# Scoring both maps of a query tile together, with their low-part products on two halves of the matrix array

## The chip, the cores and the metric

The kernel runs on one core of one Trainium2 chip. The metric is the device time of one launch in microseconds (us). TensorE (PE in the rows) does the matmuls and loads their weights (PEld); VectorE (DVE), ScalarE (ACT) and GpSimd (POOL) do the rest; SyncE (SP) starts transfers.

## The reference, cut to what matters

One inference step of two layers over 1,024 latent tokens and 128 context tokens. Each layer projects, mixes (four heads of differential attention, a Fourier branch, a gated branch) and projects back. The change sits in the attention of the latent tokens:

```python
def _diff_attention(q, k, v, lam, subln_w, lam_init):
    s = jnp.einsum('bhqmd,bhkmd->bhmqk', q, k,
                   preferred_element_type=jnp.float32) * (HEAD_DIM ** -0.5)
    p = jax.nn.softmax(s, axis=-1)
    a = p[:, :, 0] - lam * p[:, :, 1]
    o = jnp.einsum('bhqk,bhke->bhqe', a, v.astype(jnp.float32))
    ...
```

A head has two maps `m`, each with queries and keys of 64 dimensions. 1,024 queries see 1,152 keys (128 cached ones and the 1,024 latent tokens).

## The kernel before, in words

**Two-part numbers.** Matmuls run on `float32r` operands, and each operand is split into a high part (its rounding to `float32r`) and a low part (the rest). A product is then high by high, high by low and low by high.

**Scores.** For a head and a map, `K[:, m]` holds the high parts of the 64 key dimensions in one half of the 128 rows and the low parts in the other half (`split_k`, L435 to L440). `Q[:, m]` holds the high part of the query twice, in both halves (`pack`, L615 to L622). One matmul of `Q` by `K` over 128 rows thus gives two of the three products. The third, low query by high key, uses `qlo`, which holds the low part in the half where the keys' high parts stand and zeros in the other half (`low`, L625 to L630), so it too runs over 128 rows. `score` (L632) makes one map of one tile of 128 queries: three matmuls of 384 keys with `Q`, three with `qlo`, all added up in a PSUM tile `S` of three banks (L638). Then VectorE takes the negated maximum (`nm`, L640), and ScalarE the exponential and its sum (`P`, L642).

**From scores to values.** `softmax_diff` (L583 to L585): a reciprocal on VectorE, one scaling of the second map on GpSimd (`P`, L584), one multiply-and-add on VectorE (`P`, L585). `transpose` (L652): nine transposes into a PSUM tile `T`, read by ScalarE (high part, L655) and VectorE (low part `a`, L656). `values` (L662), once for two tiles: 27 matmuls into a PSUM tile `pv`, finished by `finish_o` (L594 to L604).

**PSUM.** `S`, `T` and `pv` take turns in a ring of two buffers of three banks each (`psS`), so each waits until the one before the last has been read. The other two banks (`psM`) are a ring of two for the projections' `z` and for small tiles.

**The order on TensorE** is written out by hand (`manual_schedule`). `attention` is a generator which goes over 32 tiles of a layer (eight for each of four heads). In step n it scores tile n, takes the values of a finished pair if there is one (odd n), and transposes tile n-1. At each `yield` the loop around it puts in "fill": groups of three matmuls (486 in its own units) of the projections `z` of the next heads, later of the other branches (`zt`). `FILL` is the amount for each head, `SHARE` the factor for each kind of place. `fill.until` puts in all that is missing of a projection that a head needs. At the same places one step of a head's small context attention (`prompt`, tiles `sp`, `atp`, `pvp`) is put in from the list `side`, and from the third head on `MFILL` units of modulation work on VectorE. The other engines' orders come from a scheduler, which puts what is marked `high_priority` first.

Of the kernel before, what the change touches and what calls it, by code (L numbers as in the profile page):

```python
# [10 lines left out]
F32 = mybir.dt.float32  # L11
# [12 lines left out]
CH = 384  # L24
# [5 lines left out]
SWAP = [k ^ 16 for k in range(32)]  # L30

PACE = 2
SHARE = [0.75, 1.25, 1, 1]
EARLY, LATE = 200, 0
MODS_POOL = (1, 4, 7)
MHEAD = 2
MFILL = 450
TAIL = 4
START_X = (1, 2, 0, 0, 0, 0, 0, 6)
START_W = (0, 0, 1, 2, 0, 0, 0, 0)  # L40
# [8 lines left out]

X_TAGS = {"wr": ("wraw", "woraw", "wada", "tabr", "mr", "ba"), "z": ("zz", "sh", "gt", "vT", "gmt", "gmg", "fot", "vs", "bd", "pqp", "ws", "kc", "vc", "Pp", "modacc"), "Q": ("Q", "bdr", "wsr", "h32"),
          "sq": ("sq", "wft", "dftp", "msq", "bds", "cb")}
X_BUFS = {"wr": 2, "z": 3, "Q": 2, "sq": 3, "X": 2}
X_TAGS = {n: t for t, names in X_TAGS.items() for n in names}

# [1 line left out]
def f(ap):  # L58
    return ap.bitcast(F32)
# [3 lines left out]
def backbone_step(ctx, tc, xs, xp, cT, w_ada, b_ada, w_in, w_out, ckT, cv, lamv, wf, wsT, bsT,  # L63
# [61 lines left out]
    neglam = cp.tile([128, L], F32, name="neglam")  # L125
    subs = cp.tile([128, L], F32, name="subs")

    qlo = [cp.tile([128, 2, 128], F32R, name=f"qlo{i}") for i in range(2)]
    qps = [cp.tile([128, 2, 128], F32, name=f"qp{i}") for i in range(2)]
    for t in qlo + qps:  # L130
        pool.memset(t if t.dtype == F32 else f(t), 0.0)

    def silu_c():
        sp.dma_start(cb, cT)
# [245 lines left out]
    def mm_dims(w, c, late=None):  # L380

        z = psM((128, CH), "z")
        n = 0
        for kt in range(KT):
            for a, b in ((0, 0), (0, 1), (1, 0)):
                pe.matmul(z, lhsT=w[:, a, kt, :], rhs=Hc[c][:, b, kt, :], start=n == 0, stop=n == 23)  # L386
                n += 1
            if kt == 3 and late:
                late()
            yield 486  # L390
        return z

    def mm_tok(w, ts):
# [122 lines left out]
        def chunk(self, c, z):  # L516
            silu_to(self.gs[:, c * CH:(c + 1) * CH], z, tX([128, CH], "gt"))

    finished = set()

    class Units:

# [84 lines left out]
    class Head:  # L607
# [7 lines left out]
        def pack(self, p):  # L615

            qr, qs = self.qr, slice(p * 256, p * 256 + 256)
            Q = self.Q = tX([128, 2, 256], "Q", F32R)
            act.activation(Q[0:64, 0], qr[0:64, qs], AF.Copy)
            act.activation(Q[64:128, 0], qr[0:64, qs], AF.Copy)  # L620
            act.activation(Q[64:128, 1], qr[64:128, qs], AF.Copy)
            act.activation(Q[0:64, 1], qr[64:128, qs], AF.Copy)  # L622
            return Q

        def low(self, i, Q):  # L625

            ql = slice((i % 2) * 128, (i % 2) * 128 + 128)
            for m in range(2):
                r = slice(64 * m, 64 * m + 64)
                pool.tensor_tensor(qlo[i % 2][r, m], self.qr[r, i * 128:(i + 1) * 128], f(Q[r, m, ql]), op=ALU.subtract)  # L630

        def score(self, Q, i, m, zz):  # L632
            S, K = psS(), self.K
            ql = slice((i % 2) * 128, (i % 2) * 128 + 128)

            for e, q in enumerate((Q[:, m, ql], qlo[i % 2][:, m])):
                for n in range(3):
                    pe.matmul(S[:, n, :CH], lhsT=q, rhs=K[:, m, n * CH:(n + 1) * CH], start=e == 0, stop=e == 1)  # L638
            nm = small([128, 1], "nm", 4)
            dve.tensor_reduce(nm, S[:, :, :CH], axis=AX.XY, op=ALU.max, negate=True)  # L640
            P = tP(name="P")
            act.activation(P.rearrange("p (c k) -> p c k", c=3), S[:, :, :CH], AF.Exp, bias=nm,  # L642
                           accum_out=zz[:, m:m + 1])
            return P

        def transpose(self, i, a):
            if i % 2 == 0:
# [22 lines left out]
        def prompt(self):  # L670

            l = self.l
            nm = small([128, 2], "nmp", 2)
            zz = small([128, 2], "zzp", 2)
            P = tX([128, 2, 128], "Pp")
            for m in range(2):
                S = psM((128, 128), "sp")
                pe.matmul(S, lhsT=self.qp[:, m], rhs=self.kp, start=True, stop=True)
                dve.tensor_reduce(nm[:, m:m + 1], S, axis=AX.X, op=ALU.max, negate=True)
                act.activation(P[:, m], S, AF.Exp, bias=nm[:, m:m + 1], accum_out=zz[:, m:m + 1])  # L680
                yield 0.5 * PACE
# [7 lines left out]
            pv = psM((128, 2, 128), "pvp")  # L689
            pe.matmul(pv[:, 0], lhsT=self.vp, rhs=aT, start=True, stop=True)  # L690
            sq = square_o(pv[:, 0], 128)
            yield 0.5 * PACE
            finish_o(l, pv[:, 0], pv[:, 1], sq, 128, self.gs, slice(SEQ_S, TOK))

    def attention(l, fill):

# [4 lines left out]
        for n in range(8 * H + 2):  # L701
            h, i = min(n // 8, H - 1), n % 8
            if n < 8 * H:
                if i == 0:
                    fill.until((l, U_K + h), (l, U_Q + h), (l, U_V + h))
                    hd = Head(l, h)
                    Qn = hd.pack(0)
                    hd.low(0, Qn)
                if i % 2 == 0:
                    Q = Qn  # L710
                zz = small([128, 2], "zz2", 4)
                with tc.high_priority(offset=EARLY):
                    p1 = hd.score(Q, i, 0, zz)
                if i < 7:
                    hd.low(i + 1, Qn)
                with tc.high_priority(offset=EARLY):
                    side.fill(1)
                yield h, 0
                with tc.high_priority(offset=EARLY):
                    p2 = hd.score(Q, i, 1, zz)  # L720
                if i % 2 == 0 and i < 6:
                    Qn = hd.pack(i // 2 + 1)
                with tc.high_priority(offset=EARLY):
                    side.fill(1)
                yield h, 1
            if done:
                if done[1] == 0:
                    fill.until((l, U_G + done[0].h))
                    done[0].begin_values()
                with tc.high_priority(offset=EARLY):  # L730
                    finish = done[0].values(done[1])
                with tc.high_priority(offset=EARLY):
# [421 lines left out]
```

## Time and profile before

| | |
|---|---|
| median of 3 runs | 1440.45 us (1434.82 to 1440.82) |
| the profiled execution | 1439.59 us, of which the span from first to last instruction is 1437.7 us |
| TensorE busy in the span | 93% |
| VectorE, ScalarE, GpSimd busy | 63%, 52%, 55% |
| mean granted TensorE clock | 0.979 |

The span leaves out 1.9 us of the execution. A busy TensorE counts pipelined matmuls from their start to a modelled end, so its spacing from start to start says more than its busy time.

### The profile page before, as it was taken

The numbers are of one execution on the slowest core, as the hardware profiler recorded it, in microseconds if no ns is written. First come the engines' busy times: TensorE is split into PE (matmuls) and PEld (weight loads), VectorE is DVE, ScalarE is ACT, GpSimd is POOL, SyncE is SP. The second block draws the span as 40 slices with busy tenths as digits, with TensorE's granted clock in tenths as the row PEclk, the third lists the DMA queues.
The fourth block names the chain that finished last, engine by engine and source line by source line (L and its number), as shares of the span: only waits on it lengthen the run. The fifth ranks groups of instructions, "written<-read, shape, count | busy, mean of one in ns | idle before, by whom it ended". The sixth has DMA issues, their size and how long they took to land. (4 is left out here: it accounts for less than half of the span.)

```text
span 1437.7 us, 21298 instructions
## 1 busy us (share of the span) xinstructions
PE 1330.9 (93%) x8264; PEld 1236.6 (86%) x8264; DVE 907.6 (63%) x1354; ACT 746.6 (52%) x1380; POOL 793.4 (55%) x723
## 2 busy tenths in 40 slices
PE   6899998889899999999997989989799999999997
PEld 4689998879788998987887989988789999998786
DVE  3646667787877865355785565668775684435576
ACT  3576666557454444353656565755565544435320
POOL 2455657567563446336687676575575343533752
PEclk9999999999999999999999999999999999999999
DMA  9310102211220221363341100112020010126432
GB/s 337 147 49 17 35 18 65 75 46 36 88 76 22 98 74 42 108 211 114 124 161 45 50 19 32 49 44 80 32 65 3 30 47 30 47 78 221 154 133 80
DMA packets 56158, 114.43 MB, mean 80 GB/s; under 512 B 4973, under 2 KB 32493, under 8 KB 55929
## 3 DMA queue, kind: packets, MB, share of 16 engines
q1 hardware_dynamic: 56056, 113.07, 23.7%
q8 instruction: 65, 1.06, 0.3%
q14 instruction: 37, 0.30, 0.1%
HBM read 95.47 MB, written 17.58 MB: 79 GB/s over the span
## 5 line engine op out<-in xcount | busy, mean ns | idle before, releaser
L386 PE MATMUL z<-H,w 128*128 128x384 f32 x2520 | 499.8, 345 | 22.4 <-DVE V L506 5.0
L386 PEld LDWEIGHTS z<-H,w 128*128 128x128 f32 x2520 | 444.9, 193 | 29.0 <-ACT vT L492 4.9
L642 ACT ACTIVATE P<-S,nm 128x1152 f32<-128x1152 f32 x128 | 156.4, 1222 | 118.6 <-DVE nm L640 112.1
L640 DVE TENSOR_REDUCE nm<-S 128x1 f32<-128x1152 f32 x128 | 172.3, 1349 | 40.4 <-PE S L638 39.9
L401 PE MATMUL zt<-whi,H 128*128 128x256 f32 x1152 | 158.7, 285 | 4.8 <-ACT ug L767 3.4
L401 PEld LDWEIGHTS zt<-whi,H 128*128 128x128 f32 x1152 | 147.0, 192 | 7.5 <-ACT ug L767 4.0
L584 POOL TENSOR_SCALAR P<-P,rz,neglam 128x1152 f32<-128x1152 f32 x64 | 86.8, 1356 | 98.3 <-DVE rz L583 87.2
L585 DVE SCALAR_TENSOR_TENSOR P<-P,rz 128x1152 f32<-128x1152 f32 x64 | 105.2, 1643 | 42.3 <-POOL P L584 42.3
L630 POOL TENSOR_TENSOR qlo<-qr,Q 64x128 fp32r<-64x128 f32 x128 | 81.4, 641 | 86.8 <-PE S L638 80.2
L367 POOL TENSOR_TENSOR w<-wraw,w 128x1024 fp32r<-128x1024 f32 x36 | 89.6, 2489 | 65.4 <-ACT w L366 64.9
L638 PE MATMUL S<-K,Q 128*128 128x384 f32 x384 | 93.2, 351 | 21.4 <-DVE a L656 11.0
L662 PE MATMUL pv<-a,V 128*128 128x256 f32 x864 | 109.2, 283 | 3.1 <-ACT P L642 3.1
L662 PEld LDWEIGHTS pv<-a,V 128*128 128x128 f32 x864 | 106.6, 191 | 5.1 <-ACT P L642 5.1
L656 DVE TENSOR_TENSOR a<-T,a 128x1152 fp32r<-128x1152 f32 x64 | 86.6, 1353 | 37.5 <-ACT a L655 37.4
L638 PEld LDWEIGHTS S<-K,Q 128*128 128x128 f32 x384 | 67.6, 194 | 29.8 <-DVE a L656 12.8
L638 PE MATMUL S<-K,qlo 128*128 128x384 f32 x384 | 89.7, 342 | 0.0
L1013 PE MATMUL y<-wob,mx 128*128 128x512 f32 (+1 forms) x342 | 88.3, 385 | 1.5 <-DVE rr L1015 1.5
L655 ACT ACTIVATE a<-T 128x1152 fp32r<-128x1152 f32 x64 | 72.3, 1130 | 28.5 <-PE T L652 28.2
L406 PE MATMUL zt<-wlo,H 128*128 128x256 f32 x576 | 82.7, 284 | 1.1 <-POOL wlo L367 1.1
L1013 PE MATMUL y<-wo,mx 128*128 128x512 f32 (+1 forms) x342 | 81.6, 382 | 0.0
L652 PE MATMUL T<-cs,P 128*128 128x128 f32 x576 | 73.9, 274 | 3.8 <-ACT P L642 3.7
L406 PEld LDWEIGHTS zt<-wlo,H 128*128 128x128 f32 x576 | 74.9, 191 | 1.5 <-POOL wlo L367 1.5
(222 smaller groups left out, 2376.9 us busy)
## 6 DMA issues: line engine op xcount, KB each, us to landing
wraw<-in_w_in_dram SPq DMA_DIRECT2D x52, 512.0 KB, 3.3
wada<-in_w_ada_dram SPq DMA_DIRECT2D x32, 512.0 KB, 3.6
wa<-in_w_ada_dram SPq DMA_DIRECT2D x8, 1024.0 KB, 13.0
woraw<-in_w_out_dram SPq DMA_DIRECT2D x16, 512.0 KB, 3.9
mr<-mix SPq DMA_DIRECT2D x18, 384.0 KB, 3.2
mix<-gs SPq DMA_DIRECT2D x8, 576.0 KB, 3.9
x<-rr SPq DMA_DIRECT2D x9, 512.0 KB, 3.6
xr<-x SPq DMA_DIRECT2D x9, 512.0 KB, 5.3
```

Source lines behind the costliest of these rows:

```text
L367: eng.tensor_tensor(lo, raw, f(hi), op=ALU.subtract)
L386: pe.matmul(z, lhsT=w[:, a, kt, :], rhs=Hc[c][:, b, kt, :], start=n == 0, stop=n == 23)
L401: pe.matmul(z[:, i, :], lhsT=Hc[c][:, a, kt, o:o + 128], rhs=w[0][:, kt, :], start=n == 0, stop=False)
L406: pe.matmul(z[:, i, :], lhsT=Hc[c][:, 0, kt, o:o + 128], rhs=w[1][:, kt, :], start=False, stop=kt == KT - 1)
L584: pool.tensor_scalar(p2, p2, rz[:, 1:2], neglam[:, l:l + 1], op0=ALU.mult, op1=ALU.mult)
L585: return dve.scalar_tensor_tensor(p1, p1, rz[:, 0:1], p2, op0=ALU.mult, op1=ALU.add)
L638: pe.matmul(S[:, n, :CH], lhsT=q, rhs=K[:, m, n * CH:(n + 1) * CH], start=e == 0, stop=e == 1)
L640: dve.tensor_reduce(nm, S[:, :, :CH], axis=AX.XY, op=ALU.max, negate=True)
L642: act.activation(P.rearrange("p (c k) -> p c k", c=3), S[:, :, :CH], AF.Exp, bias=nm, accum_out=zz[:, m:m + 1])
L656: dve.tensor_tensor(lo, T[:, :, 0:3], f(hi), op=ALU.subtract)
L662: pe.matmul(pv[:, 0, :], lhsT=self.V[:, a, kt, :], rhs=self.A[:, b, kt, :], start=kt == 0 and e == 0, stop=kt == 8 and e == 2)
L1013: pe.matmul(z, lhsT=mx[:, a, k, :], rhs=wo[kt][b][:, ns], start=i == 0, stop=i == 23)
```

## The change

Both maps of a tile are scored in one call, into both PSUM buffers of the ring: six matmuls with `Q` over all 128 rows, then six with the low part, alternating between the maps. The low part of map 0 stands in rows 0 to 63 and that of map 1 in rows 64 to 127 of a third plane `Q[:, 2]`, and a low product is a matmul over those 64 rows alone, so that two of them use different rows of the array. The low parts are made in `pack` for two tiles at once, two GpSimd instructions of 64x256 where there were four of 64x128. The places for fill are five per pair of tiles instead of seven, with other shares of the same total (7.0), and `MFILL` grows with it (7 times 450 and 5 times 630 are both 3,150). The small tile `Pp` moves to another ring, and a transposition of values (`late`) may be held back while the context attention holds a PSUM bank.

```diff
-SHARE = [0.75, 1.25, 1, 1]
+SHARE = [2, 1.3, 1.7, 0.7, 1.3]
...
-MFILL = 450
+MFILL = 630
...
-            if kt == 3 and late:
+            if kt >= 3 and late and not held:
                 late()
+                late = None
...
-            Q = self.Q = tX([128, 2, 256], "Q", F32R)
+            Q = self.Q = tX([128, 3, 256], "Q", F32R)
...
+            for m in range(2):
+                r = slice(64 * m, 64 * m + 64)
+                pool.tensor_tensor(Q[r, 2], qr[r, qs], f(Q[r, m]), op=ALU.subtract)
             return Q
 
-        def low(self, i, Q):
...
-        def score(self, Q, i, m, zz):
-            S, K = psS(), self.K
-            ql = slice((i % 2) * 128, (i % 2) * 128 + 128)
-
-            for e, q in enumerate((Q[:, m, ql], qlo[i % 2][:, m])):
+        def scores(self, Q, i, zz):
+
+            S, K = [psS() for _ in range(2)], self.K
+            ql = slice((i % 2) * 128, (i % 2) * 128 + 128)
+            for m in range(2):
                 for n in range(3):
-                    pe.matmul(S[:, n, :CH], lhsT=q, rhs=K[:, m, n * CH:(n + 1) * CH], start=e == 0, stop=e == 1)
...
+                    pe.matmul(S[m][:, n, :CH], lhsT=Q[:, m, ql], rhs=K[:, m, n * CH:(n + 1) * CH], start=True, stop=False)
+            for n in range(3):
+                for m in range(2):
+                    r = slice(64 * m, 64 * m + 64)
+                    pe.matmul(S[m][:, n, :CH], lhsT=Q[r, 2, ql], rhs=K[r, m, n * CH:(n + 1) * CH],
+                              start=False, stop=True)
...
                 with tc.high_priority(offset=EARLY):
-                    p1 = hd.score(Q, i, 0, zz)
-                if i < 7:
-                    hd.low(i + 1, Qn)
-                with tc.high_priority(offset=EARLY):
-                    side.fill(1)
-                yield h, 0
-                with tc.high_priority(offset=EARLY):
-                    p2 = hd.score(Q, i, 1, zz)
+                    p1, p2 = hd.scores(Q, i, zz)
                 if i % 2 == 0 and i < 6:
                     Qn = hd.pack(i // 2 + 1)
                 with tc.high_priority(offset=EARLY):
                     side.fill(1)
-                yield h, 1
+                yield h, 2 if done else 0
...
-                yield h, 2
+                yield h, 3
...
-                yield h, 3
+                yield h, 1 if i % 2 == 0 else 4
```

**TensorE**, the second tile of the second head (an odd tile, with values `pv`). Before, each map's six matmuls stand apart, with fill between them and after them:

```order
L638 MATMUL S<-K,Q 128x384 x3
L638 MATMUL S<-K,qlo_105 128x384 x3
L386 MATMUL z<-H_484,w_1681 128x384 x6
L638 MATMUL S<-K,Q 128x384 x3
L638 MATMUL S<-K,qlo_105 128x384 x3
L386 MATMUL z<-H_484,w_1681 128x384 x12
L662 MATMUL pv<-a,V 128x256 x27
L386 MATMUL z<-H_485,w_1681 128x384 x9
L594 MATMUL pv<-sq,cs 128x256
L652 MATMUL T<-cs,P 128x128 x9
L386 MATMUL z<-H_485,w_1681 128x384 x9
```

The same tile after the change (lines are shifted by a few; L636 is the high part of the scores, L640 the low part):

```order
L636 MATMUL S<-K,Q 128x384 x6
L640 MATMUL S<-K,Q 128x384 x6
L385 MATMUL z<-H_480,w_1639 128x384 x15
L668 MATMUL pv<-a,V 128x256 x27
L385 MATMUL z<-H_481,w_1639 128x384 x6
L596 MATMUL pv<-sq,cs 128x256
L658 MATMUL T<-cs,P 128x128 x9
L385 MATMUL z<-H_481,w_1639 128x384 x12
```

The fill of 36 matmuls has become 33 in this tile; it now stands in three places instead of four, and between `T` and the next scores there are 12 where there were 9, but the second map's scores follow the first's at once.

**VectorE**, the third tile of the third head (an even tile), from its maxima `nm` to those of the next tile. Before, the low part `a` of the previous tile's transposes stands ahead of this tile's multiply-and-add `P`:

```order
L640 TENSOR_REDUCE nm<-S 128x1 x2
L604 SCALAR_TENSOR_TENSOR gs<-msq,gs 128x256
L583 RECIPROCAL rz<-zz_2999 128x2
L417 TENSOR_TENSOR gs<-z,gt 128x384
L656 TENSOR_TENSOR a<-T,a 128x9x128
L585 SCALAR_TENSOR_TENSOR P<-P,rz 128x1152
```

After the change:

```order
L645 TENSOR_REDUCE nm<-S 128x1 x2
L585 RECIPROCAL rz<-zz_2977 128x2
L419 TENSOR_TENSOR gs<-z,gt 128x384
L587 SCALAR_TENSOR_TENSOR P<-P,rz 128x1152
L662 TENSOR_TENSOR a<-T,a 128x9x128
L431 STREAM_SHUFFLE sh<-zz 128x384
```

Here `P` now stands ahead of `a`. Among the even tiles of the first three heads that have a transpose, this is so in 6 of 11 in the first layer and in 5 of 11 in the second.

## Rows read from the trace of the kernel before

**Rows 1.** Windows over the two attention stretches: busy us of each engine, clock, DMA.
```profile
90.00:560.00 470.00, 435.97 (x2837) 417.66 (x2836) 332.55 (x458) 261.43 (x484) 275.05 (x255) 0.97 0.17 55
800.00:1260.00 460.00, 432.72 (x2896) 418.91 (x2895) 299.09 (x433) 262.00 (x490) 262.89 (x255) 0.99 0.13 41
```

**Rows 2.** Waits of TensorE, whole run: us in total, times, longest.
```profile
PE S L638 <- DVE a L656: 11.0, 3, 4.8
...
PE atp L685 <- DVE rz L583: 6.4, 4, 2.3
...
PE pv L662 <- ACT P L642: 3.1, 6, 0.5
PE z L386 <- ACT Pp L687: 2.9, 2, 1.5
...
PE atp L685 <- ACT P L642: 2.0, 2, 1.0
```

**Rows 3.** Timeline of TensorE, an even tile and the next: start us, length.
```profile
900.31 0.68 PE L638 MATMUL S<-K,Q 128*128 128x384 f32 x3
900.83 0.68 PE L638 MATMUL S<-K,qlo 128*128 128x384 f32 x3
901.35 1.20 PE L386 MATMUL z<-H,w 128*128 128x384 f32 x6
...
905.51 1.14 PE L652 MATMUL T<-cs,P 128*128 128x128 f32 x9
906.41 1.81 PE L386 MATMUL z<-H,w 128*128 128x384 f32 x9
...
910.14 0.68 PE L638 MATMUL S<-K,Q 128*128 128x384 f32 x3
```

**Rows 4.** Timeline of TensorE around matmuls on part of the array (128*32, 2*128).
```profile
34.50 1.07 PE L327 MATMUL macc<-wa,h 128*32 128x256 f32 x16
...
35.17 0.40 PE L327 MATMUL macc<-wa,h 128*32 128x256 f32 x4
35.50 0.62 PE L305 MATMUL z<-H,w 128*128 128x384 f32 x2
...
575.27 0.28 PE L401 MATMUL zt<-whi,H 128*128 128x256 f32 x1
575.48 0.41 PE L171 MATMUL modt<-cs,ba 2*128 2x2 f32 x4
575.81 0.70 PE L594 MATMUL pv<-sq,cs 128*128 128x256 f32 x2
576.16 0.47 PE L401 MATMUL zt<-whi,H 128*128 128x256 f32 x1
```

**Rows 5.** Timeline of ScalarE and VectorE in the same two tiles.
```profile
905.02 1.22 ACT L642 ACTIVATE P<-S,nm 128x1152 f32<-128x1152 f32 x1
906.14 0.19 ACT L642 ACTIVATION_READ_ACCUMULATOR P<-S,nm 128x1 f32 x1
...
906.37 0.17 DVE L583 RECIPROCAL rz<-zz 128x2 f32<-128x2 f32 x1 [0.25 <-ACT P L642]
907.86 1.36 DVE L656 TENSOR_TENSOR a<-T,a 128x1152 fp32r<-128x1152 f32 x1 [1.33 <-ACT a L655]
909.14 1.41 DVE L585 SCALAR_TENSOR_TENSOR P<-P,rz 128x1152 f32<-128x1152 f32 x1
910.46 1.35 DVE L640 TENSOR_REDUCE nm<-S 128x1 f32<-128x1152 f32 x1
```

**Rows 6.** Groups by line on GpSimd: busy us, mean ns, idle before them, releaser.
```profile
L584 POOL TENSOR_SCALAR P<-P,rz,neglam 128x1152 f32<-128x1152 f32 x64 | 86.8, 1356 | 98.3 <-DVE rz L583 87.2
...
L630 POOL TENSOR_TENSOR qlo<-qr,Q 64x128 fp32r<-64x128 f32 x128 | 81.4, 641 | 86.8 <-PE S L638 80.2
...
L440 POOL TENSOR_TENSOR K<-zz,K 64x256 fp32r<-64x256 f32 x16 | 17.2, 1074 | 1.2
```

More of the change, by code (lines that the diff above doesn't have):

```diff
@@ L48 @@
 U_Q, U_K, U_V, U_G, U_F, U_GF, U_U, U_VM, U_GM = 0, 4, 8, 12, 16, 18, 20, 22, 24
-X_TAGS = {"wr": ("wraw", "woraw", "wada", "tabr", "mr", "ba"), "z": ("zz", "sh", "gt", "vT", "gmt", "gmg", "fot", "vs", "bd", "pqp", "ws", "kc", "vc", "Pp", "modacc"), "Q": ("Q", "bdr", "wsr", "h32"),
-          "sq": ("sq", "wft", "dftp", "msq", "bds", "cb")}
+X_TAGS = {"wr": ("wraw", "woraw", "wada", "tabr", "mr", "ba"), "z": ("zz", "sh", "gt", "vT", "gmt", "gmg", "fot", "vs", "bd", "pqp", "ws", "kc", "vc", "modacc"), "Q": ("Q", "bdr", "wsr", "h32"),
+          "sq": ("sq", "wft", "dftp", "msq", "bds", "cb", "Pp")}
 X_BUFS = {"wr": 2, "z": 3, "Q": 2, "sq": 3, "X": 2}
@@ L126, in backbone_step @@
     subs = cp.tile([128, L], F32, name="subs")
-    qlo = [cp.tile([128, 2, 128], F32R, name=f"qlo{i}") for i in range(2)]
     qps = [cp.tile([128, 2, 128], F32, name=f"qp{i}") for i in range(2)]
-    for t in qlo + qps:
-        pool.memset(t if t.dtype == F32 else f(t), 0.0)
+    for t in qps:
+        pool.memset(t, 0.0)
     def silu_c():
@@ L387, in mm_dims @@
                 n += 1
-            if kt == 3 and late:
+            if kt >= 3 and late and not held:
                 late()
+                late = None
             yield 486
+        if late:
+            late()
         return z
@@ L517, in chunk @@
             silu_to(self.gs[:, c * CH:(c + 1) * CH], z, tX([128, CH], "gt"))
-    finished = set()
+    finished, held = set(), set()
     class Units:
@@ L622, in pack @@
             act.activation(Q[0:64, 1], qr[64:128, qs], AF.Copy)
-            return Q
-        def low(self, i, Q):
+            for m in range(2):
+                r = slice(64 * m, 64 * m + 64)
+                pool.tensor_tensor(Q[r, 2], qr[r, qs], f(Q[r, m]), op=ALU.subtract)
+            return Q
+        def scores(self, Q, i, zz):
+            S, K = [psS() for _ in range(2)], self.K
             ql = slice((i % 2) * 128, (i % 2) * 128 + 128)
             for m in range(2):
-                r = slice(64 * m, 64 * m + 64)
-                pool.tensor_tensor(qlo[i % 2][r, m], self.qr[r, i * 128:(i + 1) * 128], f(Q[r, m, ql]), op=ALU.subtract)
-        def score(self, Q, i, m, zz):
-            S, K = psS(), self.K
-            ql = slice((i % 2) * 128, (i % 2) * 128 + 128)
-            for e, q in enumerate((Q[:, m, ql], qlo[i % 2][:, m])):
-                for n in range(3):
-                    pe.matmul(S[:, n, :CH], lhsT=q, rhs=K[:, m, n * CH:(n + 1) * CH], start=e == 0, stop=e == 1)
[L639 to L644, printed above, removed]
+                for n in range(3):
+                    pe.matmul(S[m][:, n, :CH], lhsT=Q[:, m, ql], rhs=K[:, m, n * CH:(n + 1) * CH], start=True, stop=False)
[4 more added lines that the diff above has]
+                              start=False, stop=True)
+            ps = []
+            for m in range(2):
+                nm = small([128, 1], "nm", 4)
+                dve.tensor_reduce(nm, S[m][:, :, :CH], axis=AX.XY, op=ALU.max, negate=True)
+                P = tP(name="P")
+                act.activation(P.rearrange("p (c k) -> p c k", c=3), S[m][:, :, :CH], AF.Exp, bias=nm,
+                               accum_out=zz[:, m:m + 1])
+                ps.append(P)
+            return ps
         def transpose(self, i, a):
@@ L689, in prompt @@
             pv = psM((128, 2, 128), "pvp")
+            held.add(1)
             pe.matmul(pv[:, 0], lhsT=self.vp, rhs=aT, start=True, stop=True)
@@ L693, in prompt @@
             finish_o(l, pv[:, 0], pv[:, 1], sq, 128, self.gs, slice(SEQ_S, TOK))
+            held.clear()
     def attention(l, fill):
@@ L707, in attention @@
                     Qn = hd.pack(0)
-                    hd.low(0, Qn)
                 if i % 2 == 0:
```

## The prediction

> **What bounds the kernel now.** I read the windows first. In the two attention stretches TensorE is busy for 436.0 of 470 us and 432.7 of 460 us; VectorE, the next, for 71% and 65% [rows 1]. So attention is paced by TensorE, and what it loses there, 34 and 27 us, is waiting. The table of its waits says for what: 11.0 us for the low part `a` of the transposes, in three long waits; 6.4 and 2.0 us in front of the context attention's transpose `atp` and 2.9 us for its result `Pp`; 3.1 us in front of `pv` [rows 2]. The timeline then gives its pace: three score matmuls of 384 columns take 0.52 us from start to start, with `Q` as with `qlo`, so 0.173 us each, and the fill follows without a gap [rows 3]. A low product thus costs as much as the two others together, though half of its rows multiply zeros.
>
> The change touches three things, costed in turn: the array time of the low products, the waits of the context attention, and the waits for PSUM. The sum is made against the profiled execution (1439.6 us), which lies 0.9 us below the median of the runs shown.
>
> **The low products.** Before: six matmuls per tile, 1.04 us [rows 3]. After: three pairs on two halves of the rows. No row shows two row halves at once. The nearest is the start of the kernel, where matmuls use 32 of the 128 columns each: 16 of them, of 256 float32 columns, start from 34.50 us on, and the last four at 35.17, so a group of four takes 0.22 us [rows 4]. Two of the same type and length at full size fill 575.81 to 576.16, 0.17 us each [rows 4]. Four parts of the array therefore do run at once, and I take a pair at the pace of one, 0.52 us for three. That alone would take 0.52 us from each of 64 tiles, 33.3 us.
>
> But the same rows show what it costs to change the shape. From the last group of four at 35.17 the next full-size matmul comes at 35.50, and this first one's weights are loaded with nothing beside them: the two that begin there last 0.62 us, where two at the usual pace last 0.17 + 0.33 = 0.51 us. So 0.33 + 0.11 = 0.44 us pass where a group takes 0.22: 0.22 us lost on the way out [rows 4]. On the way in, a matmul of 256 columns starts at 575.27 and the first one of two rows at 575.48, 0.21 us later [rows 4]; at the pace above 256 columns take two thirds of 0.173, 0.12 us, so 0.09 us go, and weights of 128 columns, loaded in the open, add the same 0.11: 0.20 us. Together 0.42 us per tile. The Trainium skill says the same in "TensorEngine Tiling (Array Packing)", section Key Properties: changing the tiling mode drains the engine; and its section Theoretical Speedup allows up to twice the speed for 64 rows. By the speedup alone the term would be -33.3 us; the trace agrees with the drain.
>
> So a tile gains 0.52 - 0.42 = 0.10 us, and 64 tiles 6.4 us. The bounds: -33.3 us if the halves cost no change of shape; +27 us if a pair does not run at once (0.42 us per tile lost, nothing gained). I take -6.4, since both ends of it are read from rows of a changed shape.
>
> **The context attention.** Its steps are put in at five places per pair of tiles instead of seven, and each place now lies behind a longer piece of TensorE work. The waits that come from its chain being too young are 6.4 + 2.0 + 2.9 = 11.3 us [rows 2]. Between the second `sp` and `atp` there were 6 fill matmuls, one map's scores, 15 more and a transpose; now 21 fill matmuls, a transpose, 12 more and both maps' scores, about 3.6 + 1.0 + 2.1 + 2.0 = 8.7 us at the paces above, against 1.0 + 1.0 + 2.6 + 1.0 = 5.6. The longest of these waits is 2.3 us. I take all of it, -11.3 us; the bounds are 0 and -11.3.
>
> **PSUM.** This is what the change asks in return. `S`, `T`, `pv` share two buffers, and the second map's scores always take the buffer of the previous `T`. Before, 9 fill matmuls, a map's scores and 6 more stood between; in the rows `T` ends at 905.51 + 1.14 = 906.65 and the second map starts at 910.14, 3.49 us later, while `a` has read `T` at 907.86 + 1.36 = 909.22, 2.57 us after its end [rows 3, 5]. After, 12 fill matmuls and three of the first map's stand between: the fill starts 0.24 us before `T` ends [rows 3], and 15 x 0.173 = 2.60, so there are 2.36 us. The quickest chain is 0.21 us late.
>
> It is later where VectorE has `P` ahead of `a`. Count from the end of both maps' scores in an even tile: two maxima 2.70, the second exponential 1.22 and its sum 0.19, the reciprocal 0.17, GpSimd's scaling 1.36, `P` 1.41, `a` 1.36, in all 8.41 us [rows 5, 6]. `T` ends after 18 fill matmuls and nine transposes, at 0.06 + 3.12 + 1.14 = 4.32 us (0.06 is the 0.22 of the changed shape, less the 0.16 by which fill starts before the scores' end [rows 3]), and 2.36 us later, at 6.68, the next tile wants the buffer: 1.73 us late. The built order has `P` first in 11 of 22 even tiles of the first three heads. In some of them more fill stands around, so I take 1.5 each, 16.5 us; the other 35 of their 46 transposes cost 0.2 each, 7 us. The last head has nearly twice the fill (`FILL`), so I count no wait there. The 11.0 us that TensorE waits for `a` now [rows 2] are replaced by this: 23.5 - 11.0 = +12.5 us. The bounds: -11.0, if no chain is late; 46 x 1.73 - 11.0 = +69 us, if all are. Inside a pair, `pv` and `T` want the first map's buffer after 15 or 18 fill matmuls, 2.6 to 3.1 us; a maximum, an exponential and the handovers take 1.35 + 1.22 = 2.6 us [rows 5]: nothing added, nothing to spare.
>
> The Trainium skill warns of just this in "TensorEngine Tiling (Array Packing)", section PSUM Bottleneck: tiling speeds up TensorE but not the evacuation of PSUM. The trace agrees, with 2.57 us for `T` against 2.36 us of room.
>
> **At nothing:** GpSimd's low parts. 128 instructions of 0.64 us become 64 of about 1.07 us by the nearest shape [rows 6], some 69 us for 81; they are not on TensorE's path. What they do is stand in GpSimd's queue: before, it was idle for 80.2 us in front of `qlo` until TensorE had finished scores [rows 6], because the two `qlo` tiles were reused; scalings behind it waited too. That is gone, and could make `P` earlier; I price it at 0, and the lower bound of the PSUM term holds it. `Pp` in another ring, the held-back transposition and the modulation work at fewer places: 0, covered by the fill.
>
> **Sum.** -6.4 - 11.3 + 12.5 = -5.2: 1434.4 us for the profiled execution, 1435 us beside the median. A change under 0.5% (7 us) can't be told from none with this kernel.
>
> **Rivals.**
> - *No late chain.* With GpSimd's queue freed, `P` is done before `a` asks, and the PSUM term is its lower bound: -6.4 - 11.3 - 11.0 = -28.7, 1412 us. For it: the 80.2 us. Against it: the 0.21 us that even the quickest chain lacks.
> - *The shape changes for nothing.* The two halves go on without draining: -33.3 - 11.3 + 12.5 = -32, 1408 us. Against it: both places in rows 4.
> - *Slower: evacuation under load.* VectorE is busy for 71% and serves the fill as well. With 46 transposes and 24 values that now have no room, each 0.1 us of lateness beyond mine costs 7 us. The sum turns slower by 0.5% from 0.18 us on; with 0.5 us, half of an instruction of VectorE, it is +35: 1470 us. Against it: when TensorE waits, the others catch up.
> - *Slower: the halves do not run at once.* +27 - 11.3 + 12.5 = +28: 1469 us.
>
> **Chances.** My forecast's own case 0.38 (1428 to 1444), no late chain 0.20, no drain 0.12, evacuation under load 0.22, halves one after the other 0.08. Of my own case a quarter lies under 1433, so faster by over 0.5%: 0.20 + 0.12 + 0.09 = 0.41; within 0.5%: 0.30, with the mildest of the evacuation case shared out: slower 0.29. The range of 8 in 10 reaches from the faster cases to where the evacuation case is half done: 1409 to 1460 us.
>
> **What would show it.** The low products: in the changed trace, pairs that start within some 10 ns, three pairs in about 0.52 us, and a gap of some 0.2 us on either side; pairs 0.17 us apart, or no gap, refute the first term. The context attention: waits at `atp` and for `Pp` gone. PSUM: waits of the scores on `a` of some 23 us in all, most of them after even tiles, about 1.5 us long; if TensorE waits much longer for `nm` and `P` too, the evacuation case holds. I am wrong above all if the drain is not what rows 4 seem to show, or if the other engines' orders fit the new places better or worse than an order without times can tell.

## The result, and the profile after

The changed kernel takes 1494.1 us (1488.0 to 1502.0) beside 1440.0: slower, by a ratio of 1.0387 (95% interval 1.0329 to 1.0445). The forecast was 1435 us in a range of 1409 to 1460. The profiled execution took 1491.3 us, its span is 51.9 us longer than before, and the two stretches from a layer's first to its last score account for 51.6 of that.

The head of the page after: busy us, share of the span, instructions.

```profile
span 1489.6 us, 21217 instructions
...
PE 1334.8 (90%) x8264; PEld 1201.1 (81%) x8264; DVE 897.8 (60%) x1354; ACT 745.3 (50%) x1380; POOL 772.2 (52%) x657
```

The same windows as in [rows 1], after. TensorE is busy for less of them and every other engine does less too: nobody became busier, work was late.

```profile
90.00:560.00 470.00, 414.66 (x2629) 377.65 (x2628) 307.08 (x443) 245.58 (x462) 248.48 (x214) 0.95 0.17 52
800.00:1260.00 460.00, 407.51 (x2611) 374.73 (x2612) 280.74 (x426) 246.80 (x473) 243.53 (x221) 0.98 0.12 36
```

What TensorE waited for after, whole run (us in total, times, longest), against [rows 2]:

```profile
PE vt L501 <- ACT msq L600: 32.7, 6, 9.1
PE S L636 <- DVE a L662: 28.0, 21, 3.2
PE T L658 <- ACT P L647: 14.1, 6, 4.9
...
PE pv L668 <- ACT P L647: 8.5, 7, 2.9
...
PE S L636 <- ACT P L647: 1.9, 2, 1.7
```

Three lines of the same table before, which [rows 2] leave out:

```profile
PE S L638 <- ACT P L642: 5.2, 4, 1.8
PE S L638 <- ACT msq L598: 5.0, 3, 2.4
...
PE T L652 <- ACT P L642: 3.7, 2, 1.9
```

Gone are the 8.4 us in front of `atp`, the 5.0 behind `msq` and 3.3 of S for P. The fill's wait for the context attention's result `Pp` is not gone: 2.9 us [rows 2] have become 4.0. New are 32.7 us in front of `vt`, the transposition of values, which waited for `msq` nowhere before; S waits 17.0 us more for `a`, T 10.4 and pv 5.4 us more for P. The balance of the lines shown is +48.8 us, and TensorE's idle time in the two stretches grows by 47.4 of their 51.6 us (the sums stand with e3 and e4 below).

Of S's 21 waits for `a`, 16 with 24 of the 28.0 us stand in front of an odd tile, that is after an even one, as the prediction said. T's 14.1 us are another matter: two waits, of 4.88 and 4.95 us, make up most of them. The first one after:

```profile
317.14 0.79 PE L640 MATMUL S<-K,Q 64*128 64x384 f32 x6
...
320.22 2.70 DVE L435 TENSOR_TENSOR qr<-zz,sh 128x384 f32<-128x384 f32 x1 [0.91 <-POOL zz L433]
...
323.39 2.61 DVE L645 TENSOR_REDUCE nm<-S 128x1 f32<-128x1152 f32 x2
...
326.14 2.18 PE L658 MATMUL T<-cs,P 128*128 128x128 f32 x9 [4.88 <-ACT P L647]
```

The scores end at 317.93, but VectorE takes their maxima only from 323.39 on: in its queue the rotation of queries (`qr`), which waits for GpSimd, stands ahead of them. So this wait comes from VectorE's order, and not from both maps being ready at the end.

The low products after, in a timeline of TensorE (start us, length, and in brackets idle time before):

```profile
937.84 1.21 PE L636 MATMUL S<-K,Q 128*128 128x384 f32 x6
...
938.97 0.47 PEld L640 LDWEIGHTS S<-K,Q 64*128 64x128 f32 x6 [0.25 <-POOL zz L433]
938.97 0.79 PE L640 MATMUL S<-K,Q 64*128 64x384 f32 x6
...
939.69 0.64 PEld L385 LDWEIGHTS z<-H,w 128*128 128x128 f32 x4 [0.25 <-issue]
939.69 0.79 PE L385 MATMUL z<-H,w 128*128 128x384 f32 x3
```

Six matmuls in 0.79 us: the pairs run at once, with a gap of 0.25 us ahead of the halves and another behind them. From the first score to the next fill 1.85 us pass, where two maps took 2 x 1.04 [rows 3], and the first three fill matmuls last 0.79 us instead of the 0.68 that three scores take there. So a tile saves 0.12 us, 7.7 us for 64. The array term was right.

Now one of the six waits of `vt`, in the timeline after. `pvp` is the context attention's product, `vt` the transposition that is held back while it has its PSUM bank.

```profile
269.82 4.98 PE L668 MATMUL pv<-a,V 128*128 128x256 f32 x27 [2.87 <-ACT P L647]
...
275.90 0.59 PE L596 MATMUL pv<-sq,cs 128*128 128x256 f32 x2
...
277.32 0.39 PE L596 MATMUL pvp<-sq,cs 128*128 128x128 f32 x2
...
277.46 0.77 PE L385 MATMUL z<-H,w 128*128 128x384 f32 x3
277.47 0.47 ACT L600 ACTIVATE msq<-pv,epsr 128x256 f32<-128x256 f32 x1 [2.09 <-DVE gs L597]
...
281.16 1.70 POOL L604 TENSOR_TENSOR msq<-msq,sq 128x256 f32<-128x256 f32 x1
282.90 0.37 ACT L600 ACTIVATE msq<-pvp,epsr 128x128 f32<-128x128 f32 x1 [3.18 <-POOL msq L604]
...
283.32 0.90 PE L501 MATMUL vt<-cs,vT 128*128 128x128 f32 x3 [5.09 <-ACT msq L600]
...
283.87 3.23 PE L385 MATMUL z<-H,w 128*128 128x384 f32 x9
...
301.56 3.50 PE L668 MATMUL pv<-a,V 128*128 128x256 f32 x27
```

The finish of a pair (`pv<-sq`) and that of the context attention (`pvp<-sq`) stand 1.4 us apart. Both want buffers of the ring `sq`, which has three; so ScalarE can read `pvp` only when GpSimd is done with the pair's `msq`, at 282.86. Until then `pvp` keeps one of the two banks of the ring `psM`, fill has the other, and `vt`, three fill matmuls behind, waits 5.09 us.

The waits cost more than their length. Windows after, around this wait and the one of 9.1 us (the number behind the busy times is the granted clock):

```profile
270.00:276.00 6.00, 6.00 (x36) 6.00 (x37) 3.03 (x4) 1.66 (x4) 2.18 (x2) 0.72 0.30 87
276.00:283.00 7.00, 2.23 (x17) 1.81 (x15) 5.54 (x6) 2.32 (x5) 3.06 (x3) 0.88 0.27 76
283.00:290.00 7.00, 6.68 (x28) 6.19 (x29) 4.01 (x6) 2.93 (x6) 1.34 (x3) 0.64 0.27 75
290.00:300.00 10.00, 10.00 (x65) 9.40 (x64) 6.96 (x8) 6.00 (x11) 7.08 (x3) 1.00 0.18 61
394.00:403.00 9.00, 0.05 (x1) 0.00 (x0) 3.20 (x4) 3.46 (x6) 6.68 (x5) 0.68 0.34 92
403.00:412.00 9.00, 8.30 (x30) 6.92 (x31) 8.14 (x9) 2.82 (x6) 3.90 (x4) 0.56 0.46 145
```

After a stretch in which TensorE did little or nothing, the granted clock is 0.64 and 0.56, so that much of it was at the lower level of 1.2 GHz, and 1.00 again later. Nine fill matmuls at 283.87 take 3.23 us, where nine took 1.81 [rows 3]; 27 of `pv` take 4.98 at 269.82 and 3.50 at 301.56.

### The profile page after: what moved, and what is told of

Its sections match the earlier page's. It is cut to its first block, busy times and chain, and to the rows that moved or that the text cites. A ratio compares the mean times of both kernels' runs of the same rounds, so it can differ in the third digit from the quotient of the medians.

```text
span 1489.6 us, 21217 instructions
## 1 busy us (share of the span) xinstructions
PE 1334.8 (90%) x8264; PEld 1201.1 (81%) x8264; DVE 897.8 (60%) x1354; ACT 745.3 (50%) x1380; POOL 772.2 (52%) x657
## 4 chain that ended last, share of the span: by engine, by line
PE 56%; DVE 16%; POOL 9%; ACT 8%; issue 5%; DMA 4%; SPq 2%; DVEq 0%; POOLq 0%; ACTq 0%
PE z L385 15%; PE y L1013 10%; PE zt L403 8%; PE pv L668 5%; PE zt L408 4%; PE S L636 3%; ACT P L647 3%; PE T L658 2%; PE S L640 2%; DMA wada<-in_w_ada_dram 2%; DVE P L587 2%; POOL P L586 2%; DVE nm L645 2%; DVE macc L189 2%; PE dft L923 2%
## 5 line engine op out<-in xcount | busy, mean ns | idle before, releaser
L645 DVE TENSOR_REDUCE nm<-S 128x1 f32<-128x1152 f32 x128 | 168.3, 1350 | 49.3 <-PE S L640 49.3
L587 DVE SCALAR_TENSOR_TENSOR P<-P,rz 128x1152 f32<-128x1152 f32 x64 | 101.2, 1582 | 43.5 <-POOL P L586 43.5
L668 PE MATMUL pv<-a,V 128*128 128x256 f32 x864 | 113.2, 289 | 10.1 <-ACT P L647 8.5
L668 PEld LDWEIGHTS pv<-a,V 128*128 128x128 f32 x864 | 108.2, 195 | 16.7 <-ACT P L647 13.2
L636 PE MATMUL S<-K,Q 128*128 128x384 f32 x384 | 90.0, 356 | 30.6 <-DVE a L662 28.0
L636 PEld LDWEIGHTS S<-K,Q 128*128 128x128 f32 x384 | 68.7, 197 | 41.8 <-DVE a L662 36.5
L658 PE MATMUL T<-cs,P 128*128 128x128 f32 x576 | 76.6, 280 | 14.1 <-ACT P L647 14.1
L603 POOL TENSOR_TENSOR msq<-msq,sq 128x256 f32<-128x256 f32 (+1 forms) x40 | 30.4, 759 | 108.0 <-ACT sq L602 107.8
L658 PEld LDWEIGHTS T<-cs,P 128*128 128x128 f32 x576 | 68.7, 145 | 19.7 <-ACT P L647 16.0
L627 POOL TENSOR_TENSOR Q<-qr,Q 64x256 fp32r<-64x256 f32 x64 | 56.6, 885 | 42.7 <-ACT Q L621 38.2
```

The lines of the kernel that those rows point to most:

```text
L587: return dve.scalar_tensor_tensor(p1, p1, rz[:, 0:1], p2, op0=ALU.mult, op1=ALU.add)
L636: pe.matmul(S[m][:, n, :CH], lhsT=Q[:, m, ql], rhs=K[:, m, n * CH:(n + 1) * CH], start=True, stop=False)
L645: dve.tensor_reduce(nm, S[m][:, :, :CH], axis=AX.XY, op=ALU.max, negate=True)
L658: pe.transpose(T[:, kt // 3, kt % 3, :], a[:, kt * 128:(kt + 1) * 128], ident)
L668: pe.matmul(pv[:, 0, :], lhsT=self.V[:, a, kt, :], rhs=self.A[:, b, kt, :], start=kt == 0 and e == 0, stop=kt == 8 and e == 2)
```

## The experiments

Medians in us; ratio to the kernel before on the same chip, with its 95% interval.

| run | edit | median | ratio |
|---|---|---|---|
| e3_before5 | before, five places | 1460.8 | 1.0124 (1.0084-1.0164) |
| e4_full | after, full-size low products | 1497.2 | 1.0388 (1.0352-1.0423) |
| e15_mapmajor | e4, first map ahead of the second | 1483.5 | 1.0281 (1.0248-1.0315) |
| e1_inplace | after, context attention in its own P | 1487.2 | 1.0312 (1.0276-1.0349) |
| e2_shift | after, its steps one place later | 1490.0 | 1.0334 (1.0306-1.0362) |
| e7_vtlate | e1, `vt` one place later | 1470.1 | 1.0205 (1.0172-1.0238) |
| e6_seven | e1, seven places | 1462.3 | 1.0154 (1.0111-1.0198) |
| e8_shares | e1, more fill behind T | 1461.1 | 1.0155 (1.0112-1.0197) |
| e9_fill | after, more fill in heads 0 to 2 | 1498.0 | 1.0385 (1.0347-1.0423) |
| e10_bfill | before, the same | 1466.7 | 1.0184 (1.0146-1.0221) |
| e11_s7sh | e6 and e8 together | 1458.6 | 1.0130 (1.0092-1.0168) |
| e12_all | e11 and e9's fill | 1467.9 | 1.0186 (1.0160-1.0211) |
| e5_half | before, 64-row low products, unpaired | 1469.4 | 1.0197 (1.0159-1.0234) |
| e16_s7shfull | e11, full-size low products | 1454.0 | 1.0088 (1.0073-1.0103) |
| e13_evac | e11, T read by ScalarE alone | 1539.4 | 1.0680 (1.0662-1.0698) |
| e14_bevac | before, the same | 1523.0 | 1.0559 (1.0538-1.0581) |
| e17_s7shmm | e16, first map ahead of the second | 1438.2 | 0.9980 (0.9963-0.9997) |
| e18_binp | before, context attention in its own P | 1433.1 | 0.9945 (0.9925-0.9965) |

Theory A: the context attention's finish now meets a pair's finish in the ring of three, and `vt` waits behind it. Rival B: both maps' results have to leave PSUM at once, and waits only move when one is taken away. Rival C: the halves themselves cost the time.

**The change taken apart: e3, e4, e15.** e3 gives the kernel of before five places per pair for the context attention's steps, with the held-back `vt`; the fill keeps its seven places, and `Pp` its ring (the diff is cut to the place that goes):

```diff
                 if i < 7:
                     hd.low(i + 1, Qn)
-                with tc.high_priority(offset=EARLY):
-                    side.fill(1)
                 yield h, 0
```

> Kernel of before (one map after the other, full-size low products) with the context attention's steps at five places per pair instead of seven, and the held-back transposition that these places need; Pp stays in its old ring. Theory A: the two finishes stand side by side here too, waits in front of vt of 10 to 30 us appear and the time rises by 8 to 25 us to 1448-1465; the 6.4 and 2.0 us in front of atp go. Rival B: without both maps at once nothing is short, 1432-1443.

e4 takes the halves out of the changed kernel (cut to the matmul; GpSimd's low parts per tile, `qlo`, come back too):

```diff
-                    pe.matmul(S[m][:, n, :CH], lhsT=Q[r, 2, ql], rhs=K[r, m, n * CH:(n + 1) * CH],
+                    pe.matmul(S[m][:, n, :CH], lhsT=qlo[i % 2][:, m], rhs=K[:, m, n * CH:(n + 1) * CH],
```

> Changed kernel with the low products over all 128 rows again (zero-padded qlo, made per tile as before), everything else in the changed order: isolates the halves of the array. Theory A and B: three pairs gain 0.12 us per tile, so without them the time rises by 4 to 12 us, 1496-1508 (GpSimd's 0.64 us low parts per tile come back too). Rival C (the halves cost more than they save, in gaps or in the clock): 1460-1488.

So from 1440 the five places cost 21 us. Both maps together cost another 36, but that step also brings the five places of fill with their new shares, the larger `MFILL` and `Pp`'s new ring, and no run takes these apart. The halves give back 3 us by the medians and none by the ratios (1.0388 and 1.0387). Theory A held for e3. The sums of the windows from first to last score show how; in turn before, e3, e4 and after:

```profile
sum 868.20, PE 808.03 PEld 776.64 DVE 604.42 ACT 490.25 POOL 498.79; mean PE 404.01 PEld 388.32 DVE 302.21 ACT 245.13 POOL 249.39
```
```profile
sum 894.50, PE 817.74 PEld 784.48 DVE 592.66 ACT 491.42 POOL 497.72; mean PE 408.87 PEld 392.24 DVE 296.33 ACT 245.71 POOL 248.86
```
```profile
sum 924.00, PE 821.45 PEld 783.62 DVE 590.62 ACT 488.41 POOL 490.03; mean PE 410.73 PEld 391.81 DVE 295.31 ACT 244.20 POOL 245.01
```
```profile
sum 919.76, PE 812.23 PEld 742.11 DVE 593.99 ACT 487.62 POOL 474.72; mean PE 406.12 PEld 371.06 DVE 296.99 ACT 243.81 POOL 237.36
```

With e3 TensorE's idle time grows by 16.6 us (from 60.2 to 76.8), and the same matmuls are busy for 9.7 us more, at a lower mean clock (0.968 for 0.979 over the span). From e4 to after the halves take 9.2 us from TensorE's busy time, and 5.0 us of idle time come instead. The waits of e3 have `vt` as long as after, though `Pp` is in its old ring and the maps are scored apart, and next to none for `a`. T and pv wait for P there too, T above all in two waits of 4.7 us:

```profile
PE vt L502 <- ACT msq L601: 31.4, 6, 7.3
PE T L655 <- ACT P L645: 10.3, 3, 4.7
...
PE pv L665 <- ACT P L645: 5.4, 10, 0.6
...
PE S L641 <- DVE a L659: 1.4, 1, 1.4
```

In e4 the waits for `a` are at 26.3 us: they come with scoring both maps together (and what came with it), not with the halves. e15 keeps e4 and only puts the first map's six matmuls ahead of the second's six, so that its maximum can start some 0.9 us (five matmuls) earlier:

> Changed kernel with full-size low products (1497 us in its run), in which the first map's six matmuls now come ahead of the second's six: both maps still without fill between, but the first ready 0.7 us or more earlier, as pairs do not allow. If T and pv wait (15.7 and 6.6 us there) because both maps are ready only at the end, these fall under 12 together and the time to 1482-1491. If what counts is that no fill stands between the maps, 1492-1502.

It gains 14 us: S waits 13.2 us for `a` and T 7.4 for P, where e4 had 26.3 and 15.7, and `pv` no longer waits for P; two waits of S for P grow from 0.5 to 9.9 us. Pairs of the two maps do not allow this order: they end both together.

**The context attention: e1, e2, e7, e6.** e1 frees the ring of three:

```diff
-            sq = square_o(pv[:, 0], 128)
+            sq = square_o(pv[:, 0], 128, P[:, 0])
...
-            finish_o(l, pv[:, 0], pv[:, 1], sq, 128, self.gs, slice(SEQ_S, TOK))
+            finish_o(l, pv[:, 0], pv[:, 1], sq, 128, self.gs, slice(SEQ_S, TOK), P[:, 1])
```

> Changed kernel, but the context attention writes its square and its mean square into the two halves of its own P instead of two buffers of the ring of three; nothing else. Theory A (the context attention's finish now stands next to a pair's finish, and both want that ring; the held-back transposition vt waits for the PSUM bank behind it): the 32.7 us of waits in front of vt fall under 10, the pv and score matmuls after them are granted the full clock again, and the time falls by 20 to 28 us to 1466-1474. Rival B (both maps' results have to leave PSUM at once, and the waits only move): the waits of S, T and pv take up what vt gives back, 1485-1495. Rival C (the halves of the array cost the time): 1488-1495, since nothing about them changes.

The waits of `vt` fall by 20 us, the time by 7, with intervals that overlap. S and pv took some of it back, and the mean clock was lower, not higher (0.966 for 0.971); in the two stretches TensorE's idle time fell by 14.7 us and its busy time grew by 4.7:

```profile
PE S L636 <- DVE a L662: 31.3, 19, 3.2
...
PE vt L501 <- ACT Pp L600: 12.8, 6, 3.5
PE pv L668 <- ACT P L647: 10.3, 8, 2.8
```

Theory A's mechanism stood and its price did not: where a wait is removed, TensorE can run into the next one. e2 moves all the steps by one place instead (a `yield` at the head of `prompt`):

> Changed kernel with one idle step at the head of the context attention, so that all its steps come one place later: its finish then stands behind the next tile's scores, apart from the pair's finish; the ring of three buffers stays shared. Theory A: the waits in front of vt fall under 10 us as in the run with its own buffers, 1466-1478. If it is the ring alone and not the two finishes side by side, vt keeps over 20 us, 1485 or more. Rival B: the waits move to S, T and pv, 1485-1495.

`vt` keeps 18.2 us, between the two forecasts, and the time stays at 1490, though S's waits for `a` fall to 18.4 us as well: fill and S now wait elsewhere. A place further is not far enough, and the run does not tell the ring from the neighbourhood. e7 (a `yield` ahead of `held.clear()`) and e6 (a second `side.fill(1)`, ahead of the scores) go on from e1:

> Changed kernel with the context attention's square and mean in its own P, and the held-back transposition released one place later: vt then comes when pvp has long been read. vt's 12.8 us fall under 4; if the time follows, 1474-1480; if the waits in attention are set by the slowest of several chains and only move, 1484-1489.

> Changed kernel with the context attention's square and mean in its own P (as in the first run) and, besides, two more places per pair for its steps, ahead of the scores: seven again, so that its finish lies behind a tile's scores, apart from a pair's. If the five places cost what the kernel of before lost by them (21 us), this gives it back: 1468-1478, waits in front of vt under 6 us, atp waits of a few us come back. If the loss is in the scores of both maps at once, 1482-1490 and the waits of S for a stay at some 30 us.

Both beat e1, by 17 and 25 us, more than either forecast; `vt` waits 4.7 us behind `pvp` in e7, and in e6 that wait no longer shows. In e6 the waits for `a` stay at 25.0: that part is the other loss.

**Where fill stands: e8 to e12.** e8 on top of e1:

```diff
-SHARE = [2, 1.3, 1.7, 0.7, 1.3]
+SHARE = [1.8, 1.5, 1.7, 0.5, 1.5]
```

> Changed kernel with the context attention's square and mean in its own P, and the fill shifted: 1.5 instead of 1.3 behind each transpose, taken from behind the scores of even tiles (1.8 for 2) and behind the values (0.5 for 0.7): some 0.3 us more between T and the second map's scores. If S waits for a because of where the fill stands, its 31 us fall to about 20 and the time to 1472-1482; if two maps held in PSUM leave too little room wherever the fill stands, what S gains T and pv lose: 1483-1492.

It gives more than forecast, 26 us of time. S for `a` falls from 31.3 to 14.1 us; the profiled execution, the fastest of four, also had a mean clock of 0.984 for 0.966, and in the two stretches more of its gain is busy time (15 us) than idle time (13 us). e9 raises the fill itself (`FILL = [1800, 1700, 1700, 2350]` for `[1600, 1500, 1500, 2950]`), with e10 as its control:

> Changed kernel with only the fill per place raised in the first three heads (1800, 1700, 1700 for 1600, 1500, 1500) and lowered in the last (2350 for 2950): the same work in all, 13% more room around every product of the first three heads. If S, T and pv wait because two maps held in PSUM leave too little room there, S for a falls from 28 to 10-18 us, T and pv fall too, and the time to 1465-1480, with vt's waits left. If room is not what is short, 1488-1500.

> Kernel of before with the same shift of fill from the last head to the first three: the control. It has 11 us of waits for a and under 10 us for P in all, so it gains little: 1430-1441. If it gains as much as the changed kernel does, the shift helps any order and says nothing of two maps at once.

T's waits fall to 3.2 us, but S keeps 29.7 and fill itself waits 11.4 for `vT`: no gain. And the kernel of before loses 27 us by it, with 26.1 us in front of `atp` instead of 6.4 and 2.0 [rows 2]. But the work did not stay in its place, as the forecast assumed: the stretches from first to last score hold 222 matmuls fewer in e9 and 238 fewer in e10 than in the kernels that these start from, and take 34 and 4 us less, while the rest of the execution takes 41 and 25 us more. So these two runs do not settle whether room per place is short.

> Changed kernel with the context attention in its own P, seven places for its steps, and the fill shifted behind the transposes (the edits of two runs together). If the two losses are separate, their gains of 25 and 19 us beyond or beside the 7 us of the own P add up: 1436-1447. If both runs gained from the same waits, 1453-1462.

> The same with the raised fill of the first three heads as well: all three repairs around the halves of the array. If room is what is short and the repairs add: 1422-1436, faster than before by the 8 us of the array or more. If the pairs' gain is eaten by waits that no placing of fill removes: 1440-1455.

The repairs do not add: e6 and e8 each give 25 and 26 us beyond e1, together 29. So much of what they shorten is the same. With the raised fill as well (e12), which moves 228 matmuls out of the stretches, the time is 9 us longer again, not shorter as both forecasts had it.

**The halves: e5, e16.** e5 measures the change of shape by itself: only the low products' rows are halved, nothing runs at once.

```diff
-            for e, q in enumerate((Q[:, m, ql], qlo[i % 2][:, m])):
+            r = slice(64 * m, 64 * m + 64)
+            for e, q, k in ((0, Q[:, m, ql], K[:, m]), (1, qlo[i % 2][r, m], K[r, m])):
```

> Kernel of before, in which only the low products are run on the 64 rows that are not zero, one map at a time, so that nothing runs at once: three matmuls of 64 rows between full-size ones, 128 times. If each change of shape and back costs about 0.4 us, as the changed kernel's gaps of 0.25 us on either side suggest: +40 to +55 us, 1480-1495, with such gaps twice per tile. If the gap belongs to the pairs or lies beside other work: 1436-1450.

Its timeline has the gap on either side of each map's halves:

```profile
98.38 0.68 PE L639 MATMUL S<-K,Q 128*128 128x384 f32 x3
...
98.99 0.47 PEld L639 LDWEIGHTS S<-K,qlo 64*128 64x128 f32 x3 [0.25 <-issue]
98.99 0.79 PE L639 MATMUL S<-K,qlo 64*128 64x384 f32 x3
...
99.71 0.99 PEld L386 LDWEIGHTS z<-H,w 128*128 128x128 f32 x6 [0.25 <-issue]
99.71 1.31 PE L386 MATMUL z<-H,w 128*128 128x384 f32 x6
```

From the first score to the fill 1.33 us pass instead of 1.04, and six fill matmuls last 1.31 instead of 1.20 [rows 3]: 0.40 us per map, 51 us for 128. The Trainium skill says in "TensorEngine Tiling (Array Packing)", section Key Properties, that a change of the tiling mode drains the engine; the gaps agree. But the time rises by 29.5 us only, between the two forecasts. Between first and last score the sum is

```profile
sum 897.00, PE 853.79 PEld 761.85 DVE 607.94 ACT 491.76 POOL 498.56; mean PE 426.90 PEld 380.92 DVE 303.97 ACT 245.88 POOL 249.28
```

so TensorE is busy 45.8 us longer than before, and its idle time falls from 60.2 to 43.2 us. TensorE's own time is not all that paces these stretches: a longer piece on it shortens its waits. Time that it saves may come back as waits in the same way.

> The best kernel so far (1459 us) with full-size low products: the price of the halves where the placing is repaired. With 0.12 us saved per tile, 1462-1470 without them. If the gaps of the halves and the clock eat it, 1450-1459.

They do: in the repaired kernel full-size low products take 1454.0, the halves 1458.6, with intervals that overlap a little. So the 7.7 us that pairs save at the array do not reach the time.

**Evacuation: e13, e14.** T is copied out by ScalarE twice, and GpSimd subtracts:

```diff
-            dve.tensor_tensor(lo, T[:, :, 0:3], f(hi), op=ALU.subtract)
+            c = a.rearrange("p (c k q) -> p c k q", c=3, k=3)
+            act.activation(c, T[:, :, 0:3], AF.Copy)
+            pool.tensor_tensor(lo, c, f(hi), op=ALU.subtract)
```

> The best kernel so far (own P, seven places, fill behind the transposes: 1459 us) with the transposes taken out of PSUM by ScalarE alone, in two copies, and their low part subtracted by GpSimd from SBUF; VectorE, with 1.36 us less per tile, no longer stands between T and the next scores. If what is left of the loss is the evacuation of PSUM through VectorE's queue, the 16.8 us of S for a go, T and pv (28 us) fall under 18, and the time to 1433-1448. If ScalarE's second copy and GpSimd's load only move the waits: 1453-1470.

> The same evacuation by ScalarE and GpSimd in the kernel of before, as the control: it has 11 us of waits for a, so at most that is to be had: 1428-1442. If it loses 15 us or more, the busier ScalarE and GpSimd cost elsewhere what they give here.

Some 81 us are lost in both: S waits only 4.5 us for the copy out of T, but the subtraction takes GpSimd 2.8 us where VectorE took 1.36 [rows 5], ScalarE has a second copy of 1.13 us per tile, and pv waits 32.0 us for P. How much of the loss is whose, no run separates. The subtraction's group in e13 (busy us, mean ns, idle before):

```profile
L664 POOL TENSOR_TENSOR a<-P,a 128x1152 fp32r<-128x1152 f32 x64 | 179.5, 2805 | 104.1 <-ACT P L663 95.8 <-issue 5.4 <-POOL Q L627 2.5
```

**What closes it: e17, e18.** e17 puts e15's order into e16; e18 takes only e1's edit into the kernel of before.

> The repaired kernel with full-size low products (1454 us), and the first map's six matmuls ahead of the second's, which gained 14 us where the placing was not repaired. If the 12 us that the repaired kernel still lacks come from both maps being ready only at the end, T and pv (26 us there) fall under 14 and the time to 1438-1447. If they come from the missing fill between the maps, 1450-1456.

> Kernel of before with nothing but the context attention's square and mean in its own P. Its scores wait 5.0 us for a PSUM bank behind msq, which this shortens: 1432-1439. If these waits are covered by others, or the changed order of the other engines moves them: 1438-1450.

e17, with both maps scored without fill between, is level with the kernel of before (0.9980). Beside e16 only the order of the score products differs, and it is worth 16 us: the rest of the loss went with both maps becoming ready only at the end. Its waits:

```profile
PE S L641 <- DVE a L665: 14.6, 11, 2.6
PE T L661 <- ACT P L650: 9.5, 4, 3.8
...
PE pv L671 <- ACT P L650: 5.8, 3, 2.2
```

T and pv have 15.3 us where e16 had 15.9 and 10.4; the forecast was under 14. e18 came as forecast: it is 0.55% (0.35 to 0.75%) faster than the kernel of before. S no longer waits for `msq`, and its wait for `a` is 4.1 us. It has e17's own P, so beside it e17 still lacks 5 us.

## Why the prediction was wrong, step by step

- **The low products, -6.4 us.** Right at the array: 0.12 us per tile measured, 0.10 forecast, with the gaps and the pairs as described. Wrong as time: in the sum it went one to one, and the runs give 3 us or none (e4) and none (e16).
- **The context attention, -11.3 us: the step that failed.** The waits at `atp` went, as said, those for `Pp` did not (4.0 us for 2.9). And "`Pp` in another ring, the held-back transposition and the modulation work at fewer places: 0, covered by the fill" is false for the transposition. The prediction counted how old the chain would be at its next step and not where its last step would land: beside a pair's finish, in a ring of three, with a PSUM bank held. The five places cost 21 us (e3): 32 us of the error of 59. `Pp`'s new ring has no part in e3's 31.4 us; what it does in the changed kernel no run shows, nor what the larger portions of modulation work do.
- **PSUM, +12.5 us.** The mechanism was right, and the wait of S for `a` nearly so in size (28.0 us, forecast 23.5, most of it after even tiles). The net was less so: e3 shows that with five places only 1.4 of the 11.0 us that the sum takes off were left, so that scoring both maps together brought 24.9 us (e3 to e4), twice the 12.5. Mis-sized was also "nothing added, nothing to spare" inside a pair, which names handovers and adds nothing for them: T and pv wait 15.8 us more for P. Of these 8.9 us are there in e3 with the maps apart, so at most the rest comes from both maps together. As time, the step from e3 to e4 costs 36 us; the order that ends one map first gives back 14 (e15), and 16 in the repaired kernel (e17), and other shares of fill gave 26 beside e1 (e8). The rival *evacuation under load* comes nearest, with its 1470 us alone and not on top of another loss. The Trainium skill says in "TensorEngine Tiling (Array Packing)", section PSUM Bottleneck, that tiling does not speed up the evacuation; but e4 loses as much without tiling, and the 2.57 us beside 2.36 that the prediction gives for it come from a trace without tiling.
- **The clock** had no term. The matmuls of e3 are busy 9.7 us longer than the same ones before, at a lower granted clock after long waits.
- **GpSimd's low parts** at nothing: GpSimd is busy for less of the windows than before, and no wait of TensorE names them. The rival *no late chain*, that its freed queue would make `P` early, did not come: S waits for `a` more.

Together the three steps, -11.3 to +21, +12.5 to +36 and -6.4 to -3 us, make up the error of 59 us.

Open stays why the halves gain nothing in the repaired kernel. The waits of S, T and pv are alike in e11 and e16 (45.2 and 44.1 us). The sums between first and last score, e11 and then e16:

```profile
sum 889.60, PE 816.70 PEld 743.31 DVE 576.64 ACT 485.94 POOL 482.98; mean PE 408.35 PEld 371.65 DVE 288.32 ACT 242.97 POOL 241.49
```
```profile
sum 882.10, PE 814.23 PEld 773.75 DVE 577.19 ACT 487.28 POOL 497.73; mean PE 407.12 PEld 386.87 DVE 288.60 ACT 243.64 POOL 248.86
```

With the halves TensorE is idle 5.0 us longer, as between e4 and after, and busy 2.5 us longer, though its array time is less; the mean granted clock is 0.973 and 0.980. But the fastest execution of e11, at 0.979, takes 1455.1 us, and those of e16, at 0.978 to 0.980, 1453.7 to 1455.0: with the clock alike there is no gain either. And e5, with twice as many changes of shape, has 0.980 too, so that a clock that falls with the halves is not shown.

## What to carry to other kernels

Where steps are put in at fewer places, follow each chain to its last step and list what stands beside it then: which ring, which bank, who is held back behind it. Two results that become ready together need their buffers emptied together; a saving at the array is worth only what the emptying lets through, and an experiment that lengthens the array's work (e5) shows that its time does not count one to one. A wait that is removed is not a gain until the run says so: 20 us of waits gave 7. An edit that is meant to move work inside a stretch is checked by counting the instructions in it (e9, e10).

## What the runs showed of the hardware

- Two matmuls on 64 rows each run at once at the pace of one: six in 0.79 us, weights included, where three unpaired ones of e5 take 0.79 us too, with 0.25 us of gap on either side and 0.40 us lost per change and return.
- After waits of 5 and 9 us the next 7 to 9 us had a granted clock of 0.64 and 0.56; the work behind a wait took up to 1.8 times as long (3.23 for 1.81 us).
- GpSimd took 2.8 us to subtract 1152 elements per partition, VectorE 1.36. The Trainium skill gives 2.6 cycles of 1.2 GHz per element for it in "GPSIMD Engine Reference", section Elementwise — side-by-side cycle accounting: an estimate of 2.5 us; the trace has 0.3 more. With it VectorE's `P` slowed from a mean of 1.60 us (e11) to 1.88 (e13). The Trainium skill states in "SBUF — State Buffer", section Who interferes with whom, that VectorE and GpSimd contend for one port pair; the slower `P` agrees, and no run here separates that from other causes.
